# Seven-product units written as a pipeline over three engines

## The chip, the cores and the metric

The kernel runs on one core of one Trainium2 chip. The time is that of one execution on the device, in microseconds. The profile is of one such execution; "us" stands for microseconds, PE, DVE, ACT, POOL and SP for the tensor, vector, scalar, GpSimd and sync engines, and PEld for the loading of PE's weights.

## The reference

A trunk of two layers over x of 512 tokens and width 1024, float32. Each layer has a token mixer (stick-breaking attention in layer 0, a gated chunk MLP in layer 1) and a feed-forward block (FFN), each between two norms and with shift, scale and gate from a vector c. The change is in the FFN, whose width is 2816:

```python
def swiglu(h, w_gate, w_up, w_down):
    return (jax.nn.silu(h @ w_gate) * (h @ w_up)) @ w_down

shift, scale, gate = ada_modulation(c, ffn_ada_w[i], ffn_ada_b[i])
h = rms_norm(x, ffn_pre_g[i]) * (1.0 + scale) + shift
y = swiglu(h, ffn_w_gate[i], ffn_w_up[i], ffn_w_down[i])
x = x + gate * rms_norm(y, ffn_post_g[i])
```

ada_modulation multiplies silu(c) by a matrix of 1024 x 3072 and splits the result in three.

## The kernel before

**Numbers.** Every matmul operand is kept as two parts, a high one (rounded by ACT: `wh`, `Sh`, `hTh`) and a low one (what is left, by DVE: `wl`, `Sl`, `hTl`), and `mm3` (L101) issues three matmuls for each product of 128 rows: high times high, high times low, low times high. `split` (L109) makes the two parts, one instruction on ACT and one on DVE.

**The FFN.** The 2816 columns are 22 blocks of 128, f = 0 to 21, each with its gate and its up weights. The first three (`unit`) are plain. The other 19, f = 3 to 21, are done by `seven` (L1070): gate and up for both halves of the tokens are eight products of half the depth, and a scheme of the Strassen kind (Winograd's form) gets them from seven, with sums of blocks of the weights and of the activations. A product is 4 depth blocks of `mm3`, 12 matmuls with 256 columns each. The sums of activations (S "1" to "4") are made once ahead of the loops. The sums of weights are made for each unit by `blocks` (L175) from two loaded tiles xr and yr:

- x (xr itself, holds B11 and B22), b21 (half of yr), T1 and T3 (`f13` = xr + half of yr), T2 and T4 (`f24`, two sums out of f13, xr and yr), each split in a high and a low part.

A unit uses three PSUM banks R1, R2, R3, in this order: A11 B11 into R1 (ACT copies R1, "s1"), A12 B21 into R2 (DVE adds: gate, low half), S1 T1 into R3 (ACT copies it, "s5"), S2 T2 onto R1 (ACT copies it, "u1"), S4 B22 onto R3 (DVE subtracts: up, low half), S3 T3 onto R1 (DVE subtracts: up, high half), and A22 T4 onto R1, here called the closing product (ACT: Silu, gate, high half). Then DVE multiplies gate and up into `act`, the join. In the profile's names the ACT copies are e<-r, the DVE reads gu<-r,e and, for the up high half, gu<-e,r. The closing product writes on R1 and so waits for that gu<-e,r.

**What sets the order.** The instructions are issued through a tile framework, whose scheduler moves them within each engine by priority and dependences. `order` (L82) ties an instruction behind another, and while `pe["chain"]`, `dve.chain` or `act.chain` is on, all instructions of that engine stay in the order in which the code writes them (class `Written`, L55). In the loops of seven-product units these are off: the scheduler decides. Weights are taken by `wget(src, look)` (L208), which makes the weights of the next `look` items of the stream ahead of need; `seven` asks with look 1, so the weights of unit f+1 are written ahead of unit f. Loads (`wload`, `block_loads`) go out on SP's queue, two buffers for xr and two for yr. Weight tiles rotate over six pairs of buffers, three per unit.

**Background.** `Bg` computes a gate vector of the modulation meanwhile. In 12 of the 19 units (`if f % 3`) one step of it is run: for eight of them a row `G<-rawada,sc,G` on DVE (units 5, 7, 8, 10, 11, 13, 14, 16) with a load of 512 KB, then the split of G (`acch` by ACT, `accl` by DVE; the first half in f=16, the second in f=19) and wide matmuls that sum it (adaps).

The whole is bracketed in each layer by the plain units before and by the down projection after (`out_proj` in layer 0, `last` in layer 1).

## Time and profile before

| | us |
|---|---|
| median of 3 runs | 1108.36 (1106.95 to 1108.99) |
| profiled execution | 1108.13 |
| its span, first to last instruction | 1106.4 |
| PE busy | 1084.0 |
| DVE busy | 901.6 |
| ACT busy | 602.1 |
| mean granted PE clock | 0.996 |

The page's rows of groups give an instruction's line, engine and kind, output and inputs by the program's names, count, busy time and mean length in ns, then the idle time of that engine just before such instructions and what ended it. Rows of a timeline give the start in us, the length, the engine and the instruction, and in brackets the idle time before it and what ended that. Rows of the busy times by stretches give the stretch, its length, then busy time (and count) of PE, PEld, DVE, ACT and POOL, then the granted clock of PE, the share of the DMA engines and GB/s. Some matmul records are missing from the trace. The loops of seven-product units lie near 292 to 482 us in layer 0 and 795 to 985 us in layer 1.

### The profile page before, as it was taken

What the parts mean: (1) busy time and instruction counts of PE and PEld (TensorE: products, weight loads), DVE (VectorE), ACT (ScalarE), POOL (GpSimd) and SP (SyncE); (2) the same over time, 40 slices, a digit from 0 to 9 for tenths busy, and PEclk for the clock granted to TensorE, in tenths of its full rate; (3) what the DMA queues carried; (4) which work ended last, traced back from release to release, by engine and by line L of the source; (5) the groups of instructions that cost most, each with busy time, mean ns of one, the idle gap of its engine ahead of it and who ended that gap; (6) DMA issues with size and microseconds to landing.
All of it is one profiled execution on the core that took longest, in us unless ns stands there. A gap on an engine that the chain in (4) does not pass through costs nothing.

```text
span 1106.4 us, 18286 instructions
## 1 busy us (share of the span) xinstructions
PE 1084.0 (98%) x7318; PEld 977.9 (88%) x7318; DVE 901.6 (81%) x1161; ACT 602.1 (54%) x977; POOL 39.7 (4%) x71
## 2 busy tenths in 40 slices
PE   6999999999999999999999999999999999999997
PEld 5788878779999999988878988989999999989896
DVE  7777889759988989797587774759988998889986
ACT  7646767646555555562244634537555555556552
POOL 0220111000000000010000000000000000000000
PEclk9999999999999999999999999999999999999999
DMA  9676445453344444378875583333244444223233
GB/s 358 233 233 175 143 147 159 143 191 134 97 133 153 150 138 133 97 231 270 280 248 188 165 293 96 114 125 137 82 153 131 137 134 153 77 76 114 97 91 157
DMA packets 51298, 176.09 MB, mean 159 GB/s; under 512 B 5643, under 2 KB 6155, under 8 KB 50318
## 3 DMA queue, kind: packets, MB, share of 16 engines
q1 hardware_dynamic: 45166, 153.95, 42.4%
q0 software_dynamic: 6048, 20.98, 5.9%
q8 instruction: 57, 0.93, 0.3%
q14 instruction: 27, 0.22, 0.1%
HBM read 164.43 MB, written 8.39 MB: 156 GB/s over the span
## 4 chain that ended last, share of the span: by engine, by line
PE 68%; DVE 18%; DMA 6%; ACT 4%; issue 4%; SPq 0%; DVEq 0%; ACTq 0%
PE r L90 22%; PE y L90 10%; PE X L90 7%; PE v L90 7%; PE pqk L90 7%; PE u L90 4%; DVE f L64 4%; DVE wl L64 3%; DMA rawada<-in_ada 3%; PE M L90 3%; PE z L90 2%; DMA raw<-in_wdown 2%; PE av L90 2%; DVE G L64 2%; PE tw L98 2%
## 5 line engine op out<-in xcount | busy, mean ns | idle before, releaser
L64 ACT ACTIVATE wh<-raw 128x1024 fp32r<-128x1024 f32 (+1 forms) x112 | 117.1, 1053 | 134.7 <-DMA raw<-in_wdown 38.2
L64 DVE TENSOR_TENSOR wl<-raw,wh 128x1024 fp32r<-128x1024 f32 (+1 forms) x112 | 134.9, 1210 | 58.3 <-ACT wh L64 58.1
L90 PE MATMUL r<-Sh,wh 128*128 128x256 f32 x608 | 168.2, 277 | 0.5 <-ACT e L64 0.5
L90 PE MATMUL r<-Sh,wl 128*128 128x256 f32 x608 | 167.9, 276 | 0.0
L90 PE MATMUL r<-Sl,wh 128*128 128x256 f32 x608 | 167.8, 276 | 0.0
L90 PE MATMUL y<-wh,as 128*128 128x512 f32 x480 | 151.7, 393 | 0.3 <-ACT as L64 0.3
L64 DVE TENSOR_TENSOR wl<-f,wh 128x1024 fp32r<-128x1024 f32 x76 | 92.8, 1221 | 35.4 <-ACT wh L64 32.2
L64 ACT ACTIVATE wh<-f 128x1024 fp32r<-128x1024 f32 x76 | 80.9, 1064 | 68.9 <-PE r L90 67.0
L90 PEld LDWEIGHTS r<-Sh,wh 128*128 128x128 f32 x608 | 114.1, 188 | 1.1 <-ACT e L64 1.1
L90 PEld LDWEIGHTS r<-Sl,wh 128*128 128x128 f32 x608 | 114.1, 188 | 0.0
L90 PEld LDWEIGHTS r<-Sh,wl 128*128 128x128 f32 x608 | 114.1, 188 | 0.0
L90 PEld LDWEIGHTS y<-wh,as 128*128 128x128 f32 x480 | 90.5, 189 | 20.0 <-ACT as L64 0.7
L90 PE MATMUL y<-wl,as 128*128 128x512 f32 x240 | 94.1, 392 | 0.0
L90 PE MATMUL r<-hTh,wh 128*128 128x256 f32 x304 | 88.2, 290 | 4.1 <-DVE gu L64 3.5
L90 PE MATMUL r<-hTl,wh 128*128 128x256 f32 x304 | 84.2, 277 | 0.0
L90 PE MATMUL r<-hTh,wl 128*128 128x256 f32 x304 | 79.3, 277 | 0.0
L90 PE MATMUL X<-wh,as 128*128 128x512 f32 (+1 forms) x272 | 75.2, 352 | 0.0
L90 PEld LDWEIGHTS r<-hTh,wh 128*128 128x128 f32 x304 | 57.0, 188 | 11.9 <-DVE gu L64 11.8
L64 ACT ACTIVATE e<-r 128x256 f32<-128x256 f32 x114 | 43.1, 380 | 44.4 <-PE r L90 43.4
L64 ACT ACTIVATE wh<-rawx 128x1024 fp32r<-128x1024 f32 x38 | 40.4, 1064 | 33.7 <-PE r L90 29.3
L90 PE MATMUL r<-hTh,b 128*128 128x256 f32 x304 | 58.0, 276 | 0.0
L90 PEld LDWEIGHTS r<-hTl,wh 128*128 128x128 f32 x304 | 57.2, 188 | 0.1
(240 smaller groups left out, 2831.6 us busy)
## 6 DMA issues: line engine op xcount, KB each, us to landing
rawada<-in_ada SPq DMA_DIRECT2D x56, 512.0 KB, 4.7
raw<-in_wdown SPq DMA_DIRECT2D x44, 512.0 KB, 4.4
rawy<-in_wy SPq DMA_DIRECT2D x38, 512.0 KB, 3.6
rawx<-in_wx SPq DMA_DIRECT2D x38, 512.0 KB, 4.4
rawada<-in_ada POOLq DMA_DIRECT2D x24, 512.0 KB, 4.3
raw<-in_wqk SPq DMA_DIRECT2D x16, 512.0 KB, 4.0
ada<-in_ada0w SPq DMA_DIRECT2D x7, 1026.0 KB, 11.0
raw<-in_wgu SPq DMA_DIRECT2D x12, 512.0 KB, 3.6
```

Of the source, the lines that this page charges most:

```text
L64: b = f(*a, **k)
L90: b = nc.tensor.matmul(o, l, r, start=start, stop=stop, skip_group_check=True)
L98: last_tp[0] = nc.tensor.transpose(o, i, ident)
```

## The change

`blocks` is cut into named parts (`block_parts`), each one instruction or two. `seven` becomes `sevens`, which runs all 19 units of a layer with the chains of PE, DVE and ACT on, so that these three engines keep the order that is written. In unit f it writes, between the seven products, the parts of unit f+1's weights: f13 and f24 after the first product, then t13, t24, b, and x last. The end of unit f-1 (the read of R1 for the up high half, the closing product, the Silu of R1, the join) is written behind the first product of unit f, the read first of all on DVE. The background step stands behind the parts of x, ahead of S4 B22. The stream's second block is made inside the first unit and no longer ahead of it (`wget(..., 0)`, and one item less of look in `Ffn.w`). In the last unit the first down weight is made in their place. No arithmetic changes.

```diff
@@ blocks @@
     def blocks(xr, yr):
 
+        parts, W = block_parts(xr, yr)
+        for n in ("xh", "xl", "bh", "bl", "f13", "t13h", "t13l", "f24", "t24h", "t24l"):
+            b = parts[n]()
+            if n == "f13":
+                order(b, ready[0])
+        return W
+
+    def block_parts(xr, yr):
+
         fp = fwork["pool"]
...
+        t = {}
+
+        def high(n, src):
+            return act.activation(t[n][0][:], src, AF.Copy)
+
+        def low(n, src):
+            return dve.tensor_tensor(t[n][1][:], src, t[n][0][:].bitcast(F32), ALU.subtract)
+
+        def xh():
+            t["x"] = wtile(KD, P, NARROW)
+            return high("x", xr[:])
+
...
+        def f24():
+            t["f24"] = f = fp.tile([P, KD, P], F32, tag="f24", bufs=1, name=nm("f24"))
+            dve.tensor_tensor(f[:, 0:4, :], t["f13"][:, 0:4, :], xr[:, 4:8, :], ALU.add)
+            return dve.tensor_tensor(f[:, 4:8, :], f[:, 0:4, :], yr[:, 0:4, :], ALU.add)
+
...
+        parts = {
+            "xh": xh, "xl": lambda: low("x", xr[:]),
+            "bh": bh, "bl": lambda: low("b", yr[:, 0:4, :]),
+            "f13": f13, "t13h": t13h, "t13l": lambda: low("t13", t["f13"][:]),
+            "f24": f24, "t24h": t24h, "t24l": lambda: low("t24", t["f24"][:]),
+        }
+
...
@@ Ffn.w @@
-                self.ws[f] = [wget(("wgu", self.li, f, e), look) for e in range(2)]
+                self.ws[f] = [wget(("wgu", self.li, f, e), look - (f + 1 == NH) * e) for e in range(2)]
@@ Ffn.seven, Ffn.run @@
-        def seven(self, f):
-            W = wget(("blocks", (self.li, f - NH)), 1)
-            R1, R2, R3 = [bank(n)[:, :256] for n in ("r1", "r2", "r3")]
+        def sevens(self, bg0):
             S = {n: (lambda k, t=self.S[n]: (t[0][:, k, :], t[1][:, k, :])) for n in "1234"}
             S["A11"] = lambda k: hB(self.hT, k, 0, 256)
             S["A12"] = lambda k: hB(self.hT, k + 4, 0, 256)
             S["A22"] = lambda k: hB(self.hT, k + 4, 256, 256)
...
             lo, hi = slice(0, 256), slice(256, T)
...
+            pe["chain"] = dve.chain = act.chain = True
+            last = None
+            W = wget(("blocks", (self.li, 0)), 0)
+            for f in range(NH, KF):
+                more = f + 1 < KF
+                if more:
+                    n = taken[0]
+                    taken[0] += 1
+                    assert len(got) == n and stream[n][3] == ("blocks", (self.li, f + 1 - NH))
+                    if len(raws) == n:
+                        wload()
+                    parts, nextW = block_parts(*raws[n])
+                    got.append(nextW)
+                    if len(raws) == n + 1 and stream[n + 1][0] is None:
+                        wload()
+                else:
+                    parts, nextW = {}, None
+                def part(*names):
+                    for n in names:
+                        if n in parts:
+                            parts[n]()
+                def product(o, a, b, start, stop, W=W):
+                    for k in range(4):
+                        h, l = S[a](k)
+                        wh, wl = W[b](k)
+                        mm3(o, wh, wl, h, l, start and k == 0, stop and k == 3)
+                R1, R2, R3 = [bank(n)[:, :256] for n in ("r1", "r2", "r3")]
+                e = fpool.tile([P, 3, 256], F32, tag="e", name=nm("e"))
+                gu = npool.tile([P, 2, T], F32, tag="n", name=nm("gu"))
+                s1, u1, s5 = [e[:, i, :] for i in range(3)]
+                def up_hi(gu=gu, s5=s5, R1=R1):
+                    dve.tensor_tensor(gu[:, 1, hi], s5, R1, ALU.subtract)
+                def close(R1=R1, product=product):
+                    product(R1, "A22", "T4", False, True)
+                def gate_hi(gu=gu, R1=R1):
+                    last_act[0] = act.activation(gu[:, 0, hi], R1, AF.Silu)
+                def joined(f=f, gu=gu):
+                    if f // 2 == len(self.act):
+                        self.act.append(slot(F32, "act"))
+                    dve.tensor_tensor(
+                        self.act[f // 2][:, f % 2, :], gu[:, 0, :], gu[:, 1, :], ALU.mult
+                    )
+                product(R1, "A11", "B11", True, False)
+                if last:
+                    last[0]()
+                part("f13", "f24")
+                if last:
+                    last[1]()
+                act.activation(s1, R1, AF.Copy)
+                part("t13h")
+                if last:
+                    last[2]()
+                part("t24h", "t13l")
+                if last:
+                    last[3]()
+                product(R2, "A12", "B21", True, True)
+                dve.tensor_tensor(gu[:, 0, lo], R2, s1, ALU.add)
+                part("bh")
                 act.activation(gu[:, 0, lo], gu[:, 0, lo], AF.Silu)
...
+                part("bl")
+                product(R3, "1", "T1", True, False)
+                act.activation(s5, R3, AF.Copy)
+                part("t24l")
+                product(R1, "2", "T2", False, False)
+                part("xh")
+                act.activation(u1, R1, AF.Copy)
+                part("xl")
+                if not more:
+                    wemit()
+                if f % 3:
+                    bg0.step(1)
+                product(R3, "4", "B22", False, True)
+                dve.tensor_tensor(gu[:, 1, lo], R3, u1, ALU.subtract)
+                product(R1, "3", "T3", False, False)
+                last = up_hi, close, gate_hi, joined
+                W = nextW
+            for step in last:
+                step()
+            pe["chain"] = dve.chain = act.chain = False
+            bg0.step(99)
 
         def run(self, bg0, bg, bg2, steps, nhT, nxt, nS=None):
             for f in range(NH):
                 self.unit(f, 256, 256)()
-            for f in range(NH, KF):
-                self.seven(f)()
-                if f % 3:
-                    bg0.step(1)
-            bg0.step(99)
+            self.sevens(bg0)
             if self.li == 1:
                 return self.last()
             out_proj(
```

On PE, where unit f=3 meets unit f=4: r1_473 is R1 of f=3 and r1_490 that of f=4 before; the first row belongs to f=4's first product, then come closing matmuls of f=3, and then f=4 goes on. Rows that repeat in the same kind are left out here and in the next block. Before:

```order
L90 MATMUL r_490_2939<-hTl_2178,wh_2543 128x256
L90 MATMUL r_473_2816<-hTh_2490,wh_2535 128x256
L90 MATMUL r_473_2816<-hTl_2491,wh_2535 128x256
L90 MATMUL r_473_2816<-hTh_2490,wl_2536 128x256
L90 MATMUL r_490_2939<-hTh_2177,wl_2544 128x256
L90 MATMUL r_491_2940<-hTh_2183,b_441_2547 128x256
```

And now (r_463 is R1 of f=3, r_480 that of f=4):

```order
L90 MATMUL r_480_2903<-hTl_2178,wh_2869 128x256
L90 MATMUL r_480_2903<-hTh_2177,wl_2870 128x256
L90 MATMUL r_463_2795<-hTh_2490,wh_2535 128x256
L90 MATMUL r_463_2795<-hTl_2491,wh_2535 128x256
L90 MATMUL r_463_2795<-hTh_2490,wl_2536 128x256
L90 MATMUL r_481_2904<-hTh_2183,b_474_2838 128x256
```

Before, the scheduler had put 11 of the 12 matmuls of the next unit's first product ahead of the closing product, and the twelfth behind it; now all 12 stand ahead.

On DVE, unit f=4, before (r_490 to r_492 are its R1 to R3; f, b and wl are parts of the weights of f=6 and f=7):

```order
L64 TENSOR_TENSOR act_2620<-gu_2820 128x512
L64 TENSOR_TENSOR gu_2943<-r_491_2940,e_2942 128x256
L64 TENSOR_TENSOR b_503_3052<-rawy_2915,b_502_3051 128x512
L64 TENSOR_TENSOR f_507_3061<-f_504_3055,rawx_2914 128x512
L64 TENSOR_TENSOR f_522_3181<-rawx_3043,rawy_3044 128x1024
L64 TENSOR_TENSOR f_507_3061<-f_507_3061,rawy_2915 128x512
L64 TENSOR_TENSOR gu_2943<-r_492_2941,e_2942 128x256
L64 TENSOR_TENSOR wl_3048<-rawx_2914,wh_3047 128x1024
L64 TENSOR_TENSOR gu_2943<-e_2942,r_490_2939 128x256
L64 TENSOR_TENSOR wl_3058<-f_504_3055,wh_3057 128x1024
L64 TENSOR_TENSOR wl_3065<-f_507_3061,wh_3064 128x1024
```

The same unit now (r_480 to r_482), from the join of f=3 on (the first b and wl are parts of f=5's weights, those behind the two reads of f=6's):

```order
L64 TENSOR_TENSOR act_2595<-gu_2799 128x512
L64 TENSOR_TENSOR gu_2907<-r_481_2904,e_2906 128x256
L64 TENSOR_TENSOR b_492_2962<-rawy_2792,b_491_2961 128x512
L64 TENSOR_TENSOR wl_2944<-f_486_2923,wh_2943 128x1024
L64 TENSOR_TENSOR wl_2993<-rawx_2791,wh_2992 128x1024
L64 TENSOR_TENSOR gu_2907<-r_482_2905,e_2906 128x256
L64 TENSOR_TENSOR gu_2907<-e_2906,r_480_2903 128x256
L64 TENSOR_TENSOR f_504_3049<-rawx_2899,rawy_2900 128x1024
L64 TENSOR_TENSOR f_505_3051<-f_504_3049,rawx_2899 128x512
L64 TENSOR_TENSOR f_505_3051<-f_505_3051,rawy_2900 128x512
L64 TENSOR_TENSOR wl_3068<-f_504_3049,wh_3067 128x1024
```

The low half of x (wl<-rawx) stood between the two reads of R3 and R1; now it stands ahead of both, and the two reads follow each other.

On DVE in unit f=16, before, around the last background row and the split of G:

```order
L64 TENSOR_TENSOR gu_4328<-r_694_4326,e_4327 128x256
L64 SCALAR_TENSOR_TENSOR G_3038<-rawada_4297,sc,G_3038 128x1024
L64 TENSOR_TENSOR gu_4328<-e_4327,r_692_4324 128x256
L64 TENSOR_TENSOR wl_4427<-rawx_4299,wh_4426 128x1024
L64 TENSOR_TENSOR wl_4437<-f_703_4434,wh_4436 128x1024
L64 TENSOR_TENSOR accl_4550<-G_3038,acch_4549 128x512
```

And now:

```order
L64 TENSOR_TENSOR wl_4501<-rawx_4283,wh_4500 128x1024
L64 SCALAR_TENSOR_TENSOR G_2997<-rawada_4256,sc,G_2997 128x1024
L64 TENSOR_TENSOR accl_4509<-G_2997,acch_4508 128x512
L64 TENSOR_TENSOR gu_4415<-r_701_4413,e_4414 128x256
L64 TENSOR_TENSOR gu_4415<-e_4414,r_699_4411 128x256
L64 TENSOR_TENSOR f_724_4559<-rawx_4407,rawy_4408 128x1024
```

The row and accl stand ahead of both reads now; before, the read of R1 came right after the row, and accl three places further on.

## The prediction

> **What bounds the kernel now.** I read the page first: one engine is busy nearly all the time, its clock is never held back, and its largest named wait lies in the loops that the change rewrites.

> ```profile
> PE 1084.0 (98%) x7318; PEld 977.9 (88%) x7318; DVE 901.6 (81%) x1161; ACT 602.1 (54%) x977; POOL 39.7 (4%) x71
> PEclk9999999999999999999999999999999999999999
> L90 PE MATMUL r<-hTh,wh 128*128 128x256 f32 x304 | 88.2, 290 | 4.1 <-DVE gu L64 3.5
> ```

> PE sets the time, so only an idle PE can be won back, and the idle that the page names is small. Busy hides part of it, because matmuls overlap. So I took next the busy time by stretches, from a layer's first matmul of unit f=3 to the first of unit f=21, and beside it the PE timeline at one place where two units meet.

> ```profile
> 292.40:470.30 177.90, 175.72 (x1504) 172.12 (x1503) 153.80 (x208) 97.41 (x163) 0.00 (x0) 1.00 0.41 133
> 794.60:972.60 178.00, 175.85 (x1505) 172.25 (x1505) 153.94 (x208) 97.56 (x163) 0.00 (x0) 1.00 0.40 127
> 380.80 0.28 PE L90 MATMUL r<-hTh,wl 128*128 128x256 f32 x1
> 381.82 0.28 PE L90 MATMUL r<-hTh,wl 128*128 128x256 f32 x1
> 382.39 0.38 PE L90 MATMUL r<-hTh,wh 128*128 128x256 f32 x1 [0.30 <-DVE gu L64]
> 382.61 0.28 PE L90 MATMUL r<-hTl,wh 128*128 128x256 f32 x1
> ```

> From 380.80 to 381.82 there are 9 steps, so undisturbed matmuls start 0.1133 us apart, a product of 12 takes 1.36 and a unit of 84 takes 9.52. A stretch holds 18 units less one closing product, 1500 matmuls: 170.0 us, and two wide ones of the background sums, some 0.23 each: 170.5. It took 177.9 and 178.0. So **7.4 us a layer are lost** while PE looks 98.8% busy. At this meeting 381.82 to 382.39 is 0.57 instead of 0.11 and the next step is 0.22: 0.57 lost in all. What DVE did then:

> ```profile
> 380.45 0.42 DVE L64 TENSOR_TENSOR gu<-r,e 128x256 f32<-128x256 f32 x1
> 380.79 1.22 DVE L64 TENSOR_TENSOR wl<-rawx,wh 128x1024 fp32r<-128x1024 f32 x1
> 381.92 0.42 DVE L64 TENSOR_TENSOR gu<-e,r 128x256 f32<-128x256 f32 x1
> 382.25 1.22 DVE L64 TENSOR_TENSOR wl<-f,wh 128x1024 fp32r<-128x1024 f32 x1
> ```

> The read of R1 (gu<-e,r) stands behind the low half of a weight (wl<-rawx), which fills DVE from 380.79. The next unit's first product fills the twelve steps to 381.93, so R1's own third product (T3) was over at 380.57, and R1 could have been read some 1.1 us sooner. The read ends at 382.34, and the closing product, which overwrites R1, starts 0.05 later. The shorter meetings are of the same kind:

> ```profile
> 312.35 0.28 PE L90 MATMUL r<-hTl,wh 128*128 128x256 f32 x1
> 312.65 0.38 PE L90 MATMUL r<-hTh,wh 128*128 128x256 f32 x1
> 312.18 0.41 DVE L64 TENSOR_TENSOR gu<-e,r 128x256 f32<-128x256 f32 x1
> ```

> The read ends at 312.59 and PE goes on at 312.65; this one costs 0.19 and 0.11 after it, 0.30. One other loss stands at the entry, in unit f=3, where ACT copies R1 and R3 late:

> ```profile
> 296.32 0.70 ACT L64 ACTIVATE e<-r 128x256 f32<-128x256 f32 x2 [0.52 <-DVE act L64]
> 296.33 0.28 PE L90 MATMUL r<-Sh,wl 128*128 128x256 f32 x1
> 296.76 0.39 PE L90 MATMUL r<-Sh,wh 128*128 128x256 f32 x1 [0.15 <-ACT e L64]
> ```

> From 296.33 to 296.76 0.32 is lost, and 0.11 after it as at the meetings: 0.43. The 18 meetings then cost 7.0 us a layer, 0.39 each, 14.0 in both.

> **The change part by part.** On PE almost nothing moves: the scheduler already had 11 or 12 of the next unit's first 12 matmuls ahead of the closing product, and no matmul is added. What changes is DVE and ACT. I worked one unit through in the new order with these rows:

> ```profile
> 374.84 1.23 DVE L64 TENSOR_TENSOR wl<-f,wh 128x1024 fp32r<-128x1024 f32 x1 [1.57 <-ACT wh L64]
> 375.98 0.68 DVE L64 TENSOR_TENSOR act<-gu 128x512 f32<-128x512 f32 x1
> 376.58 0.42 DVE L64 TENSOR_TENSOR gu<-r,e 128x256 f32<-128x256 f32 x1
> 376.92 0.68 DVE L64 TENSOR_TENSOR b<-rawy,b 128x512 fp32r<-128x512 f32 x1
> 377.52 0.69 DVE L64 TENSOR_TENSOR f<-f,rawx 128x512 f32<-128x512 f32 x1
> 378.12 1.22 DVE L64 TENSOR_TENSOR f<-rawx,rawy 128x1024 f32<-128x1024 f32 x1
> 379.25 1.28 DVE L64 SCALAR_TENSOR_TENSOR G<-rawada,sc,G 128x1024 f32<-128x1024 f32 x1
> 277.47 0.68 DVE L64 TENSOR_TENSOR fs<-c,tp 128x512 f32<-128x512 f32 x1
> 278.19 0.69 DVE L64 SCALAR_TENSOR_TENSOR fs<-fs,tp 128x512 f32<-128x512 f32 x1
> 376.69 0.38 ACT L64 ACTIVATE e<-r 128x256 f32<-128x256 f32 x1 [0.82 <-PE r L90]
> 377.04 0.42 ACT L64 ACTIVATE gu<-gu 128x256 f32<-128x256 f32 x1
> 384.34 1.06 ACT L64 ACTIVATE wh<-f 128x1024 fp32r<-128x1024 f32 x1
> 385.30 0.63 ACT L64 ACTIVATE b<-rawy 128x512 fp32r<-128x512 f32 x1
> 382.19 0.38 ACT L64 ACTIVATE e<-r 128x256 f32<-128x256 f32 x1 [0.47 <-PE r L90]
> ```

> On DVE the next instruction starts 0.08 before the last one ends (375.98 after 374.84: 1.14 for 1.23; likewise 0.60, 0.34, 1.20), but 0.04 after its end when it needs its result (278.19). ACT I count in full. A reader of a product starts 0.25 after it ends (382.19 for a product over at 381.93); a hand-over between DVE and ACT I take at 0.05, as with PE above.

> Time from the unit's first matmul; products end at 1.36 (A11), 2.72 (the last unit's close), 4.08 (R2), 5.44 (T1), 6.80 (T2), 8.16 (B22), 9.52 (T3). DVE reads R1 first, 0.25 to 0.67. Then f13 ends at 1.81, f24 at 3.28. ACT: copy of R1 to 1.99, t13's high half to 3.05, the gate of the last unit to 3.41, t24's high half to 4.47. DVE: t13 low to 4.42, the join to 5.02, the R2 sum to 5.36, b low to 5.96, t24 low to 7.10. ACT: b high to 5.10, Silu to 5.83, copy of R3 to 6.21 (PE needs it at 6.80), x high to 7.27, copy of R1 to 7.65 (PE needs it at 8.16). DVE: x low from 7.32 to 8.54; in 8 units of a layer the background row (G) to 9.74; the R3 difference; the next read of R1 ends at 10.19, or 10.42 with the row. PE wants R1 at 10.88. **So every meeting has 0.4 to 0.65 us in hand**, and the next weights are ready by 8.54 where PE needs them from 9.52. Two units with a row in succession run 0.23 later in the second, still 0.2 in hand. I take the 14.0 us as gone.

> Given back, first, in unit f=16, once a layer: behind the row stand ACT's acch and DVE's accl, now in written order ahead of the read of R1.

> ```profile
> L64 ACT ACTIVATE acch<-G x2: 612/613/614, 421.5 to 461.0; 128x512 fp32r<-128x512 f32 x2
> L64 DVE TENSOR_TENSOR accl<-G,acch x2: 682/683/684, 423.8 to 461.8; 128x512 fp32r<-128x512 f32 x2
> ```

> From 9.74: acch to 10.40, accl to 11.13, the difference, and the read ends at 11.81 instead of 10.88: 0.98 and 0.11 after it. With ACT's overlap and a reader at 0.20 it is 0.83. Between 0.83 and 1.09, so 0.96.

> Second, the entry. The second block is now made inside the first unit, not before it, which takes 6.4 us off DVE ahead of the loop (0.60 + 1.14 + 2 × 0.60 + 3 × 1.14 by the rows above). But the loop's f13 waits for the last join of the plain units (1.1 after the first matmul), so f24 ends at 3.72, t24's high half at 4.83, b's at 5.46, Silu at 5.88, and the copy of R3 at 6.26; without a close in this unit PE wants it at 5.44. That is 0.87 and 0.11, 0.98, with the sharper readings 0.66: I take 0.82 against the 0.43 before, 0.39 lost. Below nothing is excluded only if ACT runs ahead of the chain that feeds it.

> DMAs move too. SP's queue stays in order, and the loads of unit f+2 are issued when x's low half of unit f is made, near 8.5 of the unit before.

> ```profile
> rawx<-in_wx SPq DMA_DIRECT2D x38, 512.0 KB, 4.4
> ```

> Landed 4.4 later they lie about 3.4 into unit f, and f13 asks for them at the start of the next, 6 us on; a background row between them on SP costs nothing within that. If that cover went, f13 and all behind it would wait. At the two exits the closing product still has wide matmuls in front of it and the down weights' order hardly moves: nothing, plus or minus 0.3 in each.

> Sum: 14.0 − 2 × 0.96 − 2 × 0.39 = 11.3 us. The profiled execution took 1108.13 (span 1106.4): 1096.8. The median of the runs is 0.23 above it: **1097.0**.

> **Rivals.** *DVE does not overlap.* If each DVE instruction had to finish before the next began, a unit with a row would take 10.2 us of DVE, over the 9.52. The read of R1 would end at 10.83 in the first of two such units, on the edge, and 0.64 later in the second: 0.75 with its aftermath, three pairs a layer, and 0.5 more in f=16: 2.75 a layer, 5.5 in all, **1102.5**. The 1.14 start to start for a 1.23 instruction speaks against it; that such rows were seen mostly where nothing depends on the one before speaks for it. [...]

> *The wait only changes its cause.* If crossing a semaphore there costs PE a floor, the shortest meeting (0.30) would stay 36 times, 10.8 of the 14.0, and with 2.7 given back the time is 1107.9, no change. Against it: that meeting's 0.19 is explained to 0.06 by DVE's end.

> *The written order locks the engines.* Place: f24 → t24 high → b high → Silu → copy of R3 → x high → copy of R1 and x low, one chain over ACT and DVE in which nothing can be passed any more. Its slack is 0.4 to 0.7 a unit. If each link is dearer than the rows show, by 1.1 us in a unit, PE stands 0.45 and 0.11 at 36 meetings, 20.2 us for 14.0, and with the 2.7: **1117**, slower. It decides from about 0.9 us a unit. For it: DVE is at 9.2 of 9.52 in a unit with a row. Against: ACT is at 55% in these stretches (97.4 of 177.9), and the chain begins anew each unit.

> *Nothing is given back*: entry and f=16 cost no more than now, and all 14.0 are won: 1094.4.

> **How the numbers follow.** My forecast 0.67 (own range 1095.4 to 1099), nothing given back 0.13, DVE without overlap 0.10, the floor 0.04, the lock 0.06. The range 1094 to 1102.5 holds the first three. A measurement of this kernel tells no change from 0.2%, 2.2 us; the first three are faster by more: 0.90; the floor is within: 0.04; the lock slower: 0.06.

> **What would show it.** Right: the two stretches shrink to about 172.5 us, the groups r<-hTh,wh lose "DVE gu" as releaser but for one meeting a layer, and gu<-e,r starts within 0.3 us of T3's end in the DVE timeline. Wrong: PE waits for DVE gu in pairs of units with a row (no overlap); equal gaps of 0.3 with gu<-e,r long done (floor); waits for ACT e in many units (lock). The forecast fails if f13 waits for rawx or rawy, or if the stretches after the loops start to wait for the down weights.

## The result: half of what the loops won arrives

| | before | after |
|---|---|---|
| median of the runs, us | 1108.36 | 1102.09 (1099.54 to 1104.92, 7 runs) |
| profiled execution (span) | 1108.13 (1106.4) | 1100.49 (1098.6) |
| loop stretch, f=3 to f=21, layer 0 / 1 | 177.95 / 177.91 | 171.98 / 171.93 |
| last loop matmul to first matmul of the next layer's u | 129.29 | 132.05 |

The ratio is 0.9938 [0.9923, 0.9953]: 6.3 us faster, where 11.3 were forecast. 1102.1 lies inside the range of 1094 to 1102.5, almost at its end, and outside the forecast's own range of 1095.4 to 1099. It also lies on the rival "DVE does not overlap" (1102.5), for which the profile has nothing: the time alone would have misled.

From the page of the changed kernel, PE's totals and the groups that answer to those of before, and behind them the two stretches (length, then busy us and instructions of PE, PEld, DVE, ACT, POOL; granted clock; DMA):

```profile
PE 1075.1 (98%) x7318; PEld 976.4 (89%) x7318; DVE 910.0 (83%) x1161; ACT 595.2 (54%) x977; POOL 39.7 (4%) x71
L90 PE MATMUL r<-Sh,wh 128*128 128x256 f32 x608 | 168.5, 277 | 1.6 <-ACT e L64 1.6
L90 PE MATMUL y<-wh,as 128*128 128x512 f32 x480 | 151.7, 393 | 2.7 <-DVE as L64 2.7
L90 PE MATMUL r<-hTh,wh 128*128 128x256 f32 x304 | 84.3, 277 | 1.1 <-DVE gu L64 1.1
```

```profile
293.82:465.80 171.98, 171.08 (x1504) 170.60 (x1503) 160.35 (x208) 95.14 (x164) 0.00 (x0) 1.00 0.42 133
792.72:964.65 171.93, 171.07 (x1504) 170.58 (x1503) 160.36 (x208) 95.11 (x164) 0.00 (x0) 1.00 0.40 127
```

The loops gave what was forecast: 5.97 and 5.98 us, 11.95 in both. PE's wait for gu in the loops fell from 3.5 us to 1.1, all of it in f=16. But the down projection's group (y<-wh,as), 0.3 before, now waits 2.7 for DVE. The meeting of two units with a background row, as DVE saw it in layer 0:

```profile
406.02 1.28 DVE L64 SCALAR_TENSOR_TENSOR G<-rawada,sc,G 128x1024 f32<-128x1024 f32 x1
407.22 0.42 DVE L64 TENSOR_TENSOR gu<-r,e 128x256 f32<-128x256 f32 x1
407.55 0.41 DVE L64 TENSOR_TENSOR gu<-e,r 128x256 f32<-128x256 f32 x1
407.88 1.22 DVE L64 TENSOR_TENSOR f<-rawx,rawy 128x1024 f32<-128x1024 f32 x1
409.14 0.69 DVE L64 TENSOR_TENSOR f<-f,rawx 128x512 f32<-128x512 f32 x1
```

The unit's first matmul is at 407.35, so the read of R1 lies 0.20 to 0.61 into it (the working had 0.25 to 0.67), and the closing product follows at 408.70 without a gap. 34 of the 36 meetings cost nothing. The other two are f=16 (layer 1 the same at 926.5):

```profile
427.03 0.69 DVE L64 TENSOR_TENSOR accl<-G,acch 128x512 fp32r<-128x512 f32 x1 [0.70 <-ACT acch L64]
427.97 0.41 DVE L64 TENSOR_TENSOR gu<-e,r 128x256 f32<-128x256 f32 x1
427.63 0.28 PE L90 MATMUL r<-hTh,wl 128*128 128x256 f32 x1
428.44 0.39 PE L90 MATMUL r<-hTh,wh 128*128 128x256 f32 x1 [0.53 <-DVE gu L64]
299.15 0.28 PE L90 MATMUL r<-Sh,wl 128*128 128x256 f32 x1
299.80 0.38 PE L90 MATMUL r<-Sh,wh 128*128 128x256 f32 x1 [0.37 <-ACT e L64]
469.35 1.06 ACT L64 ACTIVATE wh<-raw 128x1024 fp32r<-128x1024 f32 x1 [1.54 <-DMA raw<-in_wdown]
472.62 0.40 PE L90 MATMUL adaps<-acch,ones 128*128 128x512 f32 x1
473.44 0.38 PE L90 MATMUL r<-Sh,wh 128*128 128x256 f32 x1 [0.43 <-ACT e L64]
```

427.63 to 428.44 is 0.69 over the step, and 0.11 follows: 0.80 (forecast 0.83 to 1.09). The pair at 299 is the entry, 0.53 and 0.11 (forecast 0.66 to 0.98). The pair at 472 is the last unit, 0.60 and 0.11, which the prediction did not have: ACT's copy of R3 stands behind the high half of the second down weight, for whose load ACT waited 1.54 (the row at 469.35).

Layer 0's down projection is where the rest went. Beside the splits of its 22 slabs of activations (`as`) DVE works there through 24 background rows (A1, B1, G2 by `Bg`, two a step of `out_proj`), each from a load of 512 KB into one of two buffers. The end of these rows, DVE first, then PE:

```profile
549.34 1.28 DVE L64 SCALAR_TENSOR_TENSOR G<-rawada,sc,G 128x1024 f32<-128x1024 f32 x1 [0.88 <-DMA rawada<-in_ada]
550.54 1.22 DVE L64 TENSOR_TENSOR wl<-raw,wh 128x1024 fp32r<-128x1024 f32 x1
551.68 3.69 DVE L64 TENSOR_TENSOR as<-act,as 128x512 fp32r<-128x512 f32 x6
549.37 0.40 PE L90 MATMUL y<-wl,as 128*128 128x512 f32 x1
552.42 0.73 PE L90 MATMUL y<-wh,as 128*128 128x512 f32 x2 [2.66 <-DVE as L64]
554.84 0.40 PE L90 MATMUL y<-wh,as 128*128 128x512 f32 x1
558.10 0.78 PE L90 MATMUL adaps<-accl,ones 128*128 128x512 f32 x1 [2.86 <-DVE accl L64]
```

The last row stands in DVE's queue ahead of the splits (as) that PE needs. The first row began at 478.71 here and at 478.55 before, though the loop now ends 4.7 us sooner (478.49 for 483.15): no row stands in the loop's last unit any more, where the scheduler had put two. The written order alone is not the reason: the run free_order, without it, starts the rows behind the loop too (483.80), and the run gaps, with it, starts them at 471.34. So the rows end about when they ended before (550.62, before 549.61), and PE, which came early, waits. Summed over the profiled execution, in us from before to after: the first loop matmul 1.46 later (292.36, now 293.83; 292.02 in a second profile of the same kernel, so not the change), the stretches 11.95 less, layer 0's part 2.76 more, the last units of both layers and what follows layer 1's within 0.1 of nothing together: 7.8 less in the span. That is two thirds of the 11.95 in this execution; by the medians, 6.3, it is half.

### The profile page after: what moved, and what is told of

Read it like the earlier page. It is cut to its first block, busy times and chain, and to the rows that moved or that the text cites. A ratio compares the mean times of both kernels' runs of the same rounds, so it can differ in the third digit from the quotient of the medians.

```text
span 1098.6 us, 18089 instructions
## 1 busy us (share of the span) xinstructions
PE 1075.1 (98%) x7318; PEld 976.4 (89%) x7318; DVE 910.0 (83%) x1161; ACT 595.2 (54%) x977; POOL 39.7 (4%) x71
## 4 chain that ended last, share of the span: by engine, by line
PE 81%; DVE 7%; DMA 7%; ACT 3%; issue 1%; SPq 0%; DVEq 0%; ACTq 0%
PE r L90 26%; PE y L90 11%; PE v L90 8%; PE X L90 7%; PE pqk L90 7%; PE gu L90 6%; PE u L90 4%; DMA rawada<-in_ada 3%; PE M L90 3%; DMA raw<-in_wdown 2%; PE z L90 2%; PE av L90 2%; DVE wl L64 2%; PE tw L98 2%; DVE f L64 1%
## 5 line engine op out<-in xcount | busy, mean ns | idle before, releaser
L64 DVE TENSOR_TENSOR wl<-raw,wh 128x1024 fp32r<-128x1024 f32 (+1 forms) x112 | 135.1, 1212 | 62.8 <-ACT wh L64 62.3
L64 ACT ACTIVATE wh<-raw 128x1024 fp32r<-128x1024 f32 (+1 forms) x112 | 117.1, 1052 | 127.4 <-DMA raw<-in_wdown 48.1
L90 PE MATMUL r<-Sh,wh 128*128 128x256 f32 x608 | 168.5, 277 | 1.6 <-ACT e L64 1.6
L90 PE MATMUL r<-Sh,wl 128*128 128x256 f32 x608 | 168.2, 277 | 0.0
L90 PE MATMUL r<-Sl,wh 128*128 128x256 f32 x608 | 168.1, 277 | 0.0
L90 PE MATMUL y<-wh,as 128*128 128x512 f32 x480 | 151.7, 393 | 2.7 <-DVE as L64 2.7
L90 PEld LDWEIGHTS r<-Sh,wh 128*128 128x128 f32 x608 | 114.2, 188 | 2.6 <-ACT e L64 2.5
L90 PEld LDWEIGHTS r<-Sl,wh 128*128 128x128 f32 x608 | 114.2, 188 | 0.1
L90 PEld LDWEIGHTS r<-Sh,wl 128*128 128x128 f32 x608 | 114.2, 188 | 0.0
L64 ACT ACTIVATE e<-r 128x256 f32<-128x256 f32 x114 | 43.1, 378 | 129.8 <-PE r L90 129.7
L90 PEld LDWEIGHTS y<-wh,as 128*128 128x128 f32 x480 | 90.7, 189 | 21.8 <-DVE as L64 3.1
L90 PE MATMUL y<-wl,as 128*128 128x512 f32 x240 | 94.2, 393 | 0.0
L64 DVE TENSOR_TENSOR wl<-f,wh 128x1024 fp32r<-128x1024 f32 x76 | 92.7, 1220 | 0.0
L90 PE MATMUL r<-hTh,wh 128*128 128x256 f32 x304 | 84.3, 277 | 1.1 <-DVE gu L64 1.1
L90 PE MATMUL r<-hTh,wl 128*128 128x256 f32 x304 | 84.1, 277 | 0.0
L90 PE MATMUL r<-hTl,wh 128*128 128x256 f32 x304 | 84.1, 277 | 0.0
L64 ACT ACTIVATE wh<-f 128x1024 fp32r<-128x1024 f32 x76 | 80.6, 1061 | 5.0 <-DVE f L64 3.6
L90 PE MATMUL X<-wh,as 128*128 128x512 f32 (+1 forms) x272 | 75.2, 353 | 0.0
L90 PEld LDWEIGHTS r<-hTh,wh 128*128 128x128 f32 x304 | 57.1, 188 | 1.7 <-DVE gu L64 1.6
L90 PE MATMUL r<-hTh,b 128*128 128x256 f32 x304 | 57.9, 276 | 0.0
L90 PEld LDWEIGHTS r<-hTl,wh 128*128 128x128 f32 x304 | 57.1, 188 | 0.0
L90 PEld LDWEIGHTS r<-hTh,wl 128*128 128x128 f32 x304 | 57.1, 188 | 0.0
## 6 DMA issues: line engine op xcount, KB each, us to landing
rawada<-in_ada SPq DMA_DIRECT2D x56, 512.0 KB, 5.2
raw<-in_wdown SPq DMA_DIRECT2D x44, 512.0 KB, 4.1
rawy<-in_wy SPq DMA_DIRECT2D x38, 512.0 KB, 3.5
rawx<-in_wx SPq DMA_DIRECT2D x38, 512.0 KB, 3.9
rawada<-in_ada POOLq DMA_DIRECT2D x24, 512.0 KB, 4.6
raw<-in_wqk SPq DMA_DIRECT2D x16, 512.0 KB, 4.2
raw<-in_wgu SPq DMA_DIRECT2D x12, 512.0 KB, 3.9
```

The source lines that it names most:

```text
L64: b = f(*a, **k)
L90: b = nc.tensor.matmul(o, l, r, start=start, stop=stop, skip_group_check=True)
```

## The experiments

Twelve runs, eleven further kernels and the changed one a second time, in the order of the questions. The loop column holds the stretch f=3 to f=21 of both layers, "part" the time from the last loop matmul to the next layer's first u matmul, "half clock" how long in that part the granted clock stood at 0.50. Ratios are to the kernel before in the same group (its medians 1108.4 to 1109.1).

| run | median | ratio | loops | part | half clock |
|---|---|---|---|---|---|
| before (profile) | 1108.36 | 1 | 177.95, 177.91 | 129.29 | 3.41 |
| after (profile) | 1102.09 | 0.9938 [0.9923, 0.9953] | 171.98, 171.93 | 132.05 | 3.41 |
| read_late | 1112.22 | 1.0031 [1.0018, 1.0044] | 177.02, 177.05 | 132.09 | 3.41 |
| read_first | 1104.68 | 0.9963 [0.9949, 0.9978] | 175.89, 175.38 | 129.15 | 0 |
| read_cover | 1100.26 | 0.9921 [0.9904, 0.9938] | 173.03, 172.91 | 126.96 | 0 |
| free_order | 1112.20 | 1.0031 [1.0016, 1.0046] | 178.46, 176.10 | 134.12 | 6.83 |
| after_again | 1102.99 | 0.9949 [0.9931, 0.9968] | 172.01, 171.91 | 134.23 | 6.83 |
| rows_early | 1097.45 | 0.9896 [0.9881, 0.9911] | 172.03, 171.92 | 129.05 | 0 |
| half_loads | 1092.57 | 0.9854 [0.9837, 0.9870] | 172.01, 171.91 | 125.05 | 0 |
| rows_slots | 1092.05 | 0.9849 [0.9836, 0.9863] | 171.98, 171.92 | 124.86 | 0 |
| before_slots | 1104.29 | 0.9959 [0.9944, 0.9973] | 178.25, 178.02 | 125.16 | 0 |
| gaps | 1096.00 | 0.9888 [0.9870, 0.9907] | 170.99, 171.00 | 132.58 | 10.24 |
| combo | 1094.24 | 0.9869 [0.9855, 0.9883] | 170.97, 170.97 | 128.91 | 0 |
| combo_slots | 1088.53 | 0.9817 [0.9802, 0.9833] | 171.02, 171.02 | 123.38 | 0 |

(The expectations of the first group give the changed kernel's stretch as 173.4; that window reached 13 matmuls into f=21. The stretch as defined is 172.0.)

### What makes a meeting cheap

**read_late**, the read one place back:

```diff
-                if last:
-                    last[0]()
-                part("f13", "f24")
+                part("f13")
+                if last:
+                    last[0]()
+                part("f24")
```

> The changed kernel with one instruction moved: DVE reads R1 for the up half (gu<-e,r) behind the next weight sum f<-rawx,rawy (1.26 us) and not ahead of it. Theory (the place of this read sets the loss at the meetings of two units): a unit without a background row leaves DVE idle 0.86 us ahead of the read, the sum fills that and the read still ends in time; in the 8 units of a layer with a row, and in f=16, the read then ends near 1.8 us into the unit where PE wants it at 1.36, so about 0.5 to 0.7 us and 0.11 behind it are lost at some 9 meetings a layer: 10 to 15 us in all, a median of 1112 to 1117 and stretches of 178 to 180 us from the first matmul of f=3 to that of f=21 instead of 173.4. Rival (the weights made by deadline gave the gain, the place of the read matters little): within 2 us of the changed kernel's 1102.

The median went up by 10.1 to 1112.2, the stretches by 5.0 and 5.1. Layer 0 loses 0.40 and 0.11 at seven meetings behind a unit with a row, 1.79 and 0.11 at f=16, and nothing where there is no row. One of the seven, with the read behind the sum, PE held from 410.15 to 410.66:

```profile
409.06 1.22 DVE L64 TENSOR_TENSOR f<-rawx,rawy 128x1024 f32<-128x1024 f32 x1
410.19 0.41 DVE L64 TENSOR_TENSOR gu<-e,r 128x256 f32<-128x256 f32 x1
410.15 0.28 PE L90 MATMUL r<-hTh,wl 128*128 128x256 f32 x1
410.66 0.39 PE L90 MATMUL r<-hTh,wh 128*128 128x256 f32 x1 [0.23 <-DVE gu L64]
```

One instruction, moved by one place, takes back five sixths of what the loops had won, and the time is over that of the kernel before. The theory stands; its price of 0.5 to 0.7 a meeting was a little high.

**read_first**, the kernel before with the low halves tied behind the read:

```diff
+        def behind(b):
+            if read[0] is not None:
+                order(b, read[0])
...
-        split(x[0][:], x[1][:], xr[:])
+        behind(split(x[0][:], x[1][:], xr[:]))
...
-        split(t13[0][:], t13[1][:], f13[:])
+        behind(split(t13[0][:], t13[1][:], f13[:]))
...
-        split(t24[0][:], t24[1][:], f24[:])
+        behind(split(t24[0][:], t24[1][:], f24[:]))
```

Here `split` returns DVE's low half and `read[0]` is the last unit's read of R1.

> The kernel before, scheduler and all, with one rule added: the three low halves of a block that follow the read of R1 in the queue (wl<-rawx, wl<-f, wl<-f) are ordered behind the read of the last unit begun. Nothing is written out by hand and the two weights ahead remain. Theory (the read behind a low half is the whole loss of 7.0 us a layer): the stretches shrink from 177.9 to 171 to 172 us, PE shows no wait for gu at the meetings, and the median falls to 1094 to 1098, or to 1097 to 1101 if the row chain in layer 0's down projection takes back up to 3 us there as it did in the changed kernel. Rival A (the order by deadline is needed as well: low halves that are pushed back come too late for their products): PE waits for wl instead, stretches of 175 us or more, 1104 or above. Rival B (the read is not the cause): 1108.

A miss on both sides: 2.1 and 2.5 us a layer instead of 6 to 7, 1104.7. The weights are not late: in the loop PE waits for gu, not for wl. Yet most meetings still cost 0.22 and a few 0.4 to 0.55. The row of the read and PE's steps at one of them:

```profile
409.63 0.42 DVE L64 TENSOR_TENSOR gu<-e,r 128x256 f32<-128x256 f32 x1 [0.87 <-PE r L90]
409.43 0.28 PE L90 MATMUL r<-hTh,wh 128*128 128x256 f32 x1
409.88 0.28 PE L90 MATMUL r<-hTl,wh 128*128 128x256 f32 x1
410.11 0.39 PE L90 MATMUL r<-hTh,wh 128*128 128x256 f32 x1
410.33 0.28 PE L90 MATMUL r<-hTl,wh 128*128 128x256 f32 x1
```

The unit's first product begins at 409.43, and after five of its twelve matmuls comes the closing product, at 410.11 instead of 409.99, since the read ends at 410.05. With the read out of the way, the scheduler pulled the closing product forward until it met the read again. Here a read that ended 0.06 behind the matmul's turn (409.99) cost 0.11 at this matmul and 0.11 at the next.

**read_cover**, the same with the closing product tied behind all twelve:

```diff
             product(R1, "A11", "B11", True, False)
+            last12 = pe["prev"]
+            if before:
+                before(last12)
```

`before` is the closing product of the last unit; its first matmul is ordered behind `last12`.

> The kernel before with the rule of the run read_first (low halves of a block behind the read of R1) and one more on PE: a unit's closing product starts behind all 12 matmuls of the next unit's first product, where the scheduler of read_first put it behind 5. Everything else is left to the scheduler. Theory (the loss at a meeting goes when the read comes first and 1.36 us of other matmuls lie between R1's third product and its last): no meeting costs, stretches of 170.5 to 172 us and a median of 1094 to 1099 against 1104.7 with the read alone. Rival (a meeting costs 0.22 us in any order that the scheduler makes, the three engines in written order are needed): 174 us or more a stretch, 1102 to 1105.

The loops fall to 173.0 and 172.9, 2.5 to 2.9 more than with the read alone and 1.0 short of the changed kernel's, a little above the range that the theory gave; the median of 1100.3 is 1.3 above its range too. But two rules, with DVE and ACT left to the scheduler, give five sixths of what the pipeline in written order gives in the loops. In the whole time they give more: 1100.26 against 1102.99 for the changed kernel in the same group. The part behind the loop is 126.96 here, and the first two rows stand in the loop's last unit again, from 474.27 on, 4.6 ahead of its end.

**free_order**, the changed kernel with the three engines released in the loops (the line that sets the chains is taken out).

> The changed kernel with the three engines left to the scheduler inside the loops; the pieces of the next block stay where the text has them. The scheduler then puts another instruction right ahead of the read of R1 in 30 of the 38 units, in 22 of them the low half of t13 or t24 (1.23 us). Theory (the place of the read sets the loss): the meetings cost again, up to 0.4 us each as in the kernel before, stretches of 175 to 179 us, a median of 1105 to 1110. Rival (making the pieces one unit ahead by deadline is enough): within 2 us of 1102. Beside it: with the engines free the first background rows (A<-rawada) may run before the end of layer 0's loop, and then the waits of up to 3 us in its down projection would be shorter by as much.

178.5 and 176.1: the meetings cost again, up to 0.9 each in layer 0 and 1.5 in layer 1, more than forecast, and the median of 1112.2 is over its range and over the kernel before. Making the pieces by deadline gives little without the order, 1.3 us in the two loops together. The side remark failed: the rows did start no sooner (483.80 for a loop that ended at 483.63).

### Where layer 0's share went

**after_again**, the changed kernel unaltered.

> The changed kernel once more, unaltered, beside the runs of this group. In its first profile a window of 3.41 us at half clock began at 558.1, inside layer 0's down projection, and PE waited there for the background rows at 549 and 555. If the rows are what it waits for, the waits come back in this second profile at the same place of the program (2.5 to 3.5 us each), whether or not a half-clock window lies there; if they were chance, they don't. Median 1100 to 1104.

The waits came back at the same place, the first longer (549.15 to 554.75) and the second shorter (1.1), and with them the half clock. Windows around it, the changed kernel's first profile and then this one (the figure ahead of the last two is the granted clock):

```profile
554.84:558.14 3.30, 0.44 (x3) 0.05 (x1) 3.12 (x5) 0.01 (x1) 0.00 (x0) 1.00 0.91 358
558.14:561.55 3.41, 3.41 (x8) 2.73 (x9) 3.41 (x4) 1.26 (x2) 0.00 (x0) 0.50 0.75 238
561.55:565.00 3.45, 3.45 (x16) 2.78 (x16) 2.19 (x4) 1.63 (x3) 0.00 (x0) 1.00 0.86 290
```

```profile
549.15 0.40 PE L90 MATMUL y<-wl,as 128*128 128x512 f32 x1
554.75 1.22 PE L90 MATMUL y<-wh,as 128*128 128x512 f32 x2 [5.20 <-DVE as L64]
551.28:558.11 6.83, 3.36 (x8) 2.72 (x9) 6.44 (x9) 3.21 (x6) 0.00 (x0) 0.50 0.80 256
```

PE ran 8 matmuls in 3.41 us at 0.50 and 16 in 3.45 at 1.00. So in the changed kernel's first profile the waits cost twice: themselves, and half of the 3.41 us at half clock, in which PE was busy throughout.

**rows_early**, the first two rows in the loop's last unit, where DVE idled 4.0 us:

```diff
                 if last:
                     last[0]()
                 part("f13", "f24")
+                if bg and not more:
+                    bg.step(ROWS)
```

`ROWS` is 2, and the point at which `out_proj` ends the rows comes one step sooner.

> The changed kernel with the first two background rows of layer 0's down projection (A<-rawada) computed in the loop's last unit, where DVE stands idle for 4.0 us and both rows have landed; the rows after it follow two a step as they did, so the chain of 24 starts some 10 us earlier and has one pair less behind the loop. Theory (this chain, 3.0 us a row, is what PE waits for near 549 and 555 us in layer 0's down projection): from the last loop matmul to the first matmul of the next layer's u the 132.05 us fall back to 128 to 130, the wait of 2.8 us at 549 is gone or below 1, and the median falls by 2 to 4 us, to 1098 to 1100. Rival (PE waits there for its own weights or for DVE's order, not for the rows): 131.5 to 132.5 for the part and no change of the median beyond 1 us.

The part fell to 129.05, the wait of 2.8 to 0.28, the median to 1097.45, just under its range; waits of 1.8 and 1.2 behind it remain. Of the 3.0 us of the part the half clock that is missing makes up 1.7, and the loop ends 1.45 later, since matmuls of the projection moved ahead of its end; so this run supports the theory by the vanished wait and the median, not by the size of the part.

**half_loads**, 12 of the 24 loads left out, DVE's work and order kept.

> The changed kernel with every second of the 24 background rows of layer 0's down projection computed from the row loaded before it: 12 of the 24 loads of 512 KB are left out, so these rows of the modulation are not those of the reference; DVE's 24 instructions and their order stay. Theory (the chain of rows is paced by its loads: two buffers, 4.8 us from issue to landing): the pairs come closer than 6.0 us, the last row ends before 542 instead of 550.6, PE's wait of 2.8 us near 549 goes, and the part from the last loop matmul to the next layer's first u matmul falls from 132 to 127 to 129.5 (130.4 to 127.7 where no half-clock window lies in either). Rival (DVE's work or queue order paces it): the last row still ends near 550 and the part stays within 1 us.

125.05, below the range: the last row ends at 527.8, no wait of PE over 0.4 us is left and no half clock, 1092.6. The rows are paced by their loads. Whether the loads wait for buffers or for a full queue, this run can't tell, since it takes load off the queue as well; the next one can.

**rows_slots**, all loads kept, more buffers:

```diff
-        Bg("G1", slots=True), Bg("A1", "B1", "G2"), bg2, 2, hT2,
+        Bg("G1", slots=True), Bg("A1", "B1", "G2", slots=True), bg2, 2, hT2,
```

> The changed kernel with the 24 background rows of layer 0's down projection loaded into the large pool of 4 KB slots, whose hT and S tiles are free by then, and not into two buffers; each row is loaded one step ahead of its use. All work stays. Theory (two buffers and 4.8 us from issue to landing pace the rows; the wait of PE that follows also brings a window of 3.4 us or a multiple of it at half clock): the rows come two per step of the projection (5.4 us) or faster, PE's waits near 549 and 555 fall under 1.5 us each, no half-clock window follows, the part from the last loop matmul to the next layer's first u matmul falls from 132 and 134 to 125 to 128, and the median falls by 5 to 9 us to 1093 to 1098. Rival (the DMA queues are simply full there, 0.84 busy, so that more loads in flight only wait for one another): the part stays above 130.

124.86 and 1092.05, beyond the range in the good direction. The B and G rows between 478 and 552 us in before, after and rows_slots (busy, mean ns | idle of DVE ahead of them and its releaser):

```profile
L64 DVE SCALAR_TENSOR_TENSOR G<-rawada,sc,G 128x1024 f32<-128x1024 f32 x8 | 10.3, 1285 | 8.4 <-DMA rawada<-in_ada 8.4
L64 DVE SCALAR_TENSOR_TENSOR B<-rawada,sc,B 128x1024 f32<-128x1024 f32 x8 | 10.3, 1284 | 6.8 <-DMA rawada<-in_ada 6.8
```

```profile
L64 DVE SCALAR_TENSOR_TENSOR G<-rawada,sc,G 128x1024 f32<-128x1024 f32 x8 | 10.3, 1285 | 7.8 <-DMA rawada<-in_ada 7.7
L64 DVE SCALAR_TENSOR_TENSOR B<-rawada,sc,B 128x1024 f32<-128x1024 f32 x8 | 10.3, 1284 | 7.1 <-DMA rawada<-in_ada 7.0
```

```profile
L64 DVE SCALAR_TENSOR_TENSOR B<-rawada,sc,B 128x1024 f32<-128x1024 f32 x8 | 10.3, 1283 | 0.1
L64 DVE SCALAR_TENSOR_TENSOR G<-rawada,sc,G 128x1024 f32<-128x1024 f32 x8 | 10.3, 1283 | 0.1
```

The sign was in the profile of before: DVE stood idle 15.2 us for these loads. It was easy to pass over: PE, which came later, paid for it with one half-clock window and one wait, for the split of a sum of these rows:

```profile
558.58 0.51 PE L90 MATMUL adaps<-acch,ones 128*128 128x512 f32 x1 [2.43 <-ACT acch L64]
```

The DMA queue was not full either. Its share and the loads' median time to landing, after (478 to 550) and rows_slots (478 to 532):

```profile
q1 hardware_dynamic: 5598, 20.39, 83.4%
rawada<-in_ada SPq DMA_DIRECT2D x23, 512.0 KB, 4.8
```

```profile
q1 hardware_dynamic: 5136, 18.68, 94.8%
rawada<-in_ada SPq DMA_DIRECT2D x21, 512.0 KB, 6.7
```

Each load takes longer, and more of them are under way (by these medians 21 × 6.7 us in 54 us, for 23 × 4.8 in 72): a pair of rows every 4.25 us instead of 6.0, and PE has no gap from the loop to 550:

```profile
525.51 2.60 DVE L64 SCALAR_TENSOR_TENSOR G<-rawada,sc,G 128x1024 f32<-128x1024 f32 x2
529.77 2.60 DVE L64 SCALAR_TENSOR_TENSOR G<-rawada,sc,G 128x1024 f32<-128x1024 f32 x2
478.00:550.00 72.00, 72.00 (x319) 59.59 (x318) 60.10 (x61) 29.72 (x40) 2.34 (x3) 1.00 0.84 300
```

A step of the projection is 24 of these matmuls, 24 × 72.00 / 319 = 5.4 us on PE. Two rows a step at 6.0 lose 0.6 against it; at 4.25 they don't.

**before_slots**, the same edit on the kernel before.

> The kernel before with the one edit of the run rows_slots: the 24 background rows in the pool of slots, loops untouched. It tells what the change is worth where the rows no longer bind. In the profile of before layer 0's down projection takes 129.29 us, in that of rows_slots 124.86. Theory (the rows' waits and their half-clock window are what took the change's gain back, and before pays a smaller part of them): this kernel gains 4 to 5.5 us and comes to 1103 to 1104.5, so that against rows_slots (1092.05) the change of the loops is worth 11 to 12.5 us, the 11.3 that were forecast, where it is worth 6 with two buffers. Rival (the slots help the loops as well, or the change brought the whole wait about): 1107 to 1109, or under 1101.

1104.29. With the slots on both sides the change of the loops is worth 12.2 us (1104.29 to 1092.05), and the stretches of the two profiles differ by 12.4; with two buffers it is worth 6.3. That answers where the gain went. The slots are worth 4.8 us to the kernel before, which had been paying for the rows as well, and 10 to the changed one.

### The three waits left in the loops

**gaps**, with the splits one step later, R3's copy earlier in f=3, and two down weights in the last unit's written order:

```diff
+            if self.slots:
+                yield
             for name, at, s, part in self.parts:
...
+                if not last:
+                    part("bh")
+                    act.activation(gu[:, 0, lo], gu[:, 0, lo], AF.Silu)
+                    part("bl")
...
                 if not more:
                     wemit()
+                    wemit()
```

> The changed kernel with its three remaining waits in the loops taken away: the splits of the background sums one step later (f=17, 19, 20, none in a unit with a row); in unit f=3 the copy of R3 ahead of b's high half and Silu on ACT; and in the last unit the second weight behind the loop split in written order, so that ACT no longer waits for its load ahead of the gate. By the trace of the changed kernel that is 0.80 and 0.82 at f=16, 0.64 and 0.59 at the entry, 0.71 and 0.77 in the last unit: 4.3 us over both layers. Theory (layer 0's part is taken back by the background rows behind the loop, which start no earlier): only layer 1's 2.2 us show, median 1 to 3 us under the changed kernel's. Rival (nothing takes it back): 4 to 5 us under it.

The stretches are 171.0, 0.9 and 1.0 less, and layer 1 to its first M matmul is 1.9 shorter. In layer 0's profile nothing is left of it (loops and part 317.1 us, in the two profiles of the changed kernel 316.7 and 319.0), as the theory said. The median is 6 to 7 us lower all the same, more than either expected. The rows begin 5.6 to 7.4 us sooner here (471.34), since DVE no longer waits for the second weight; whether the executions without a profile had shorter waits for it was not seen, and stays open (their granted clocks, 0.994 to 0.997 against 0.992 to 0.998 in the changed kernel, don't settle it).

**combo** (gaps and rows_early) and **combo_slots** (gaps and rows_slots):

> The edits of the runs gaps and rows_early together. Theory: 1097.5 of rows_early alone less the loops' waits of 3.7 to 4.3 us, less what the earlier weight adds to the rows' start: 1092 to 1095. Rival (rows and waits are two views of one loss, as the rows of the run gaps started 5 us earlier as well): within 1 us of 1096.

> The edits of the runs gaps and rows_slots together. Theory: the three waits in the loops (4.3 us over both layers, 0.3 of it still there at each entry) and the waits of layer 0's down projection with their half-clock window (6 to 9 us) add up now, since nothing takes the first back any more: a median of 1088 to 1093. Rival (something else in layer 0's down projection binds next, its weights or the sums of the rows on PE): within 2 us of the better of the two edits alone.

1094.24 fits the theory (1.8 under gaps and 3.2 under rows_early, so the two overlap in part). With the slots the three waits are worth 3.5 us (1092.05 to 1088.53) of their 4.3. **combo_slots is the fastest: 1088.5 us, 0.9817 [0.9802, 0.9833] of before**, 13.6 us under the change itself.

## Why the prediction was right in the loops and wrong behind them

- **The loss and its cause.** "The read of R1 stands behind the low half of a weight": right, and read_late shows it from the other side (10.1 us for one place). 14.0 forecast as gone; by the stretches 11.95 was won net of what was given back, where 11.3 was forecast. (A stretch holds 17 of the 18 meetings; the last, 0.30, lies behind its end.) The three signs of being right came: stretches of 172.0 for 172.5, a wait for gu at one meeting a layer, the read 0.20 behind T3.
- **Given back.** f=16 at 0.80 for 0.96, the entry at 0.64 for 0.82 (before 0.43): right in kind, both just under the lower end of their bounds (0.83 and 0.66).
- **"On PE almost nothing moves."** True of this change, but it hid a condition: the twelve matmuls ahead of the closing product are cover that a scheduler spends. read_first and read_cover price it at 2.5 to 2.9 us a layer.
- **The failing step: "At the two exits ... nothing, plus or minus 0.3 in each."** The last unit has a new wait of 0.7 in each layer, yet with all that follows it layer 1 comes out within 0.2 of before, so that there "nothing" held in sum. Layer 0's exit costs 2.8 (132.05 for 129.29) to 4.9 (134.23). The prediction asked what the down weights would do and not what else the next stretch was paced by. The row chain, 24 × 3.0 us from a start that did not move, is slower than PE's own 5.4 us for two rows, so that what was won ahead of it turned into a wait, with the half clock on top. Its sentence "the forecast fails if the stretches after the loops start to wait" named the sign, for the weights. That 1102.1 is inside the range all the same is luck: the upper end, 1102.5, was put there for DVE that does not overlap, and nothing of the kind took place.
- **"Its clock is never held back."** A misreading: the row of nines shows tenths of slices of 28 us, and a mean of 0.996 is not 1. The profile of before has the clock at 0.50 for 3.41 us at 559.3, in the very stretch that took the gain back.
- **Rivals.** *DVE does not overlap*: no pair of row units waits, and 406.02, 407.22, 407.55 follow each other 0.08 before the end; the row that reads the result of the one ahead of it starts 0.04 behind that one's end (409.14, after 409.10). *The floor*: 34 of 36 meetings without a gap. *The lock*: ACT is waited for at the entry and in the last unit alone. *Nothing given back*: refuted by f=16.

## What to carry to other kernels

Before a stage is made faster, look at the next one for a chain that is paced by something other than the bound engine (here DVE rows that wait 15 us for loads in two buffers, and cost PE one wait of 2.4 us so far), and work out when that chain ends against when PE will arrive. A wait is taken away by the order on both engines: the reader first in its queue, and enough other matmuls between the product and its overwriting; tie both, since a scheduler spends the cover it sees. When a gain falls short, give the suspected second bound its buffers in both kernels: the difference of the two shows the change's own worth.

## What the runs showed of the hardware

```profile
554.73:558.14 3.41, 0.55 (x4) 0.12 (x2) 3.23 (x6) 0.01 (x1) 0.00 (x0) 1.00 0.90 352
551.99:555.40 3.41, 2.12 (x7) 1.13 (x7) 3.41 (x6) 3.26 (x7) 0.00 (x0) 1.00 0.79 263
555.40:558.81 3.41, 2.01 (x9) 1.58 (x9) 2.67 (x4) 3.02 (x5) 0.00 (x0) 1.00 0.97 338
```

Right ahead of the half clock PE was busy for 0.55 us of such a stretch in the changed kernel, for 0.98 in before and for 1.46 in gaps; in read_first for 2.12 and 2.01, and in rows_early for 1.66, no half clock followed. So in these profiles the wait's length alone does not tell which wait brings the half clock: 2.59 in before did and 2.85 in read_first did not, and what differs there is how much PE worked in the stretch. The executions spread as well: the seven of the changed kernel run from 1099.54 us at a mean granted clock of 0.998 to 1104.92 at 0.992 (another at 0.992 took 1100.76), the four of rows_slots from 1091.90 to 1092.36 at 0.997 and 0.998.
